# Gate, attention and state-space projections by tokens: 512 weight columns moving instead of 256 token columns

## The chip, the cores and the metric

The kernel runs on one core of a Trainium2 chip. The metric is the device time of one execution in microseconds, taken as the median of the runs. The engines are TensorE (PE in the profile; PEld is its weight load), VectorE (DVE), ScalarE (ACT), GpSimd (POOL) and SyncE (SP, which issues the loads).

## What is computed

One decoder block on 256 tokens of width 2048, in float32. Cut to the part around the change, the reference is:

```python
h = rms_norm(x, norm_mix_g) * (1.0 + sc1) + sh1          # sc1, sh1, g1, ... = silu(c) @ w_ada + b_ada
proj = h @ w_in                                          # (256, 8192)
u, q, k, v, ga, gb = split(proj, ...)                    # 1024 each; ga and gb 2048 each
y = gelu(s5_scan(u))                                     # state-space branch, (256, 1024)
y_ssm = y * sigmoid(y @ w_glu + b_glu)
y_att = attention(q, k, v, rel_bias)                     # 8 heads of 128, causal, (256, 1024)
merged = (sigmoid(ga) * (y_ssm @ w_proj_ssm)
          + sigmoid(gb) * (y_att @ w_proj_attn))         # (256, 2048)
x = x + g1 * (merged @ w_out)
h2 = rms_norm(x, norm_mlp_g) * (1.0 + sc2) + sh2
x = x + g2 * (square(relu(h2 @ w_ff1)) @ w_ff2)
out = rms_norm(x, norm_final_g)
```

## The kernel before

Every large product is computed in split precision. A weight tile of 128 rows (one k-tile of the contraction) by 1024 columns is loaded by SyncE (`load`, line 132) into one of seven `wraw` buffers. ScalarE casts it to the high part `whi` (line 137), and VectorE subtracts to get the low part `wlo` (line 139); there are four buffers of each. The activations are split in the same way (`xh`, `xl`). Three products then make one: high by high, low by high, high by low. Such a tile of 128 by 1024 with its matmuls is called a **unit** below.

There are two ways to run a unit on TensorE:

- `gemm_t` (lines 155 to 170) keeps 128 weight columns stationary and moves the 256 tokens. The result is transposed: features on the partitions, tokens along the free axis. A unit takes 8 column blocks by 3 products, which is 24 matmuls (lines 167, 168, 169) with 256 columns moving.
- `gemm_n` (lines 199 to 223) keeps 128 tokens stationary and moves 512 weight columns. The result has tokens on the partitions. A unit takes 2 token halves by 2 column halves by 3 products, which is 12 matmuls (lines 217, 218, 219) with 512 columns moving.

Either way the results fill four PSUM banks of 128 by 512 out of five (`mm`). Three more banks (`ax`) are for everything small.

The order of the work is that of the program, with priorities, put into a fixed instruction order per engine by a scheduler that simulates the kernel before it is built. Weight loads and splits get a higher priority (`OFF`). Work beside the large products sits in "lanes" (`lane`, `step`, lines 115 to 123): after each unit every lane may release so many jobs, at rates that are written as constants. The lane `ada` streams `w_ada` through the same `wraw` buffers and reduces it on VectorE (line 273). The lane `m` carries attention, then the state-space scan.

The order of the large products is: q, k, v, u and the first 1024 columns of gate a (`ga`) in three sweeps over the k-tiles (lines 986 to 993; `ga` takes ten k-tiles in the sweep of line 986 as `(4, 0, 1)` and six as `(4, 2, 2)`, both through line 960, with the partial sum in `gp`); the other three blocks of 1024 gate columns, 16 units each (lines 1023 to 1030), beside attention and then the state-space scan; `proj_attn(0)`, 8 units (lines 1044 to 1050); the GLU product, 8 units (line 1058); `proj_attn(1)`, 8 units; the state-space projection in two column groups of 8 units (lines 1072 to 1080); `w_out` by `gemm_n`, 2 times 16 units (line 1090). After it come the second norm and the feed-forward layers.

In the kernel before, all gate and projection results come from `gemm_t` and lie feature by token. The gates are copied out of PSUM by ScalarE (line 1029), or added by VectorE (line 925), and turned into sigmoids in the lane `sig` (line 1037). `proj_attn` multiplies each bank into `gb` (line 1048). The state-space branch keeps its tokens in another order (`s c` in place of `c s`), so the multiplication of the state-space projection into `ga` reads and writes with a stride (line 1078). Then `gb` is added (line 1079) and the sum is split into `mh` and `ml` (line 1080, which runs lines 137 and 139). As `mh` already has features on its partitions, `w_out` uses it as its stationary operand without further work.

## Time and profile before

| what | value |
|---|---|
| runs | 1430.0, 1430.75, 1433.79 us; median 1430.75 us |
| profiled execution, first to last instruction (span) | 1430.7 us, 24505 instructions |
| busy share | PE 97%, PEld 88%, DVE 73%, ACT 49%, POOL 3% |
| DMA | 353.47 MB, mean 247 GB/s |
| matmuls by `gemm_t`, all stages | 896 + 512 on each of lines 167, 168 and 169 by their largest groups |

The page gives the span of the profiled execution and no other time for it. The span lies 0.05 us under the median of the runs, so sums are made against 1430.7 us. Busy time on PE counts a matmul from its start to its modelled end, and neighbours overlap, so the distance from one matmul's start to the next says what a stream costs, and the mean duration does not. "Chain" means the chain of work that ended last, followed back from the end.

### The profile page before, as it was taken

Reading aid. Unit: us, or ns where it says so; the run is one execution under the profiler, and the core shown is the slowest. Engines: PE = TensorE matmul, PEld = TensorE weight load, DVE = VectorE, ACT = ScalarE, POOL = GpSimd, SP = SyncE. Lnnn points to the kernel's source line nnn. Section 1 sums busy time; section 2 is a strip of 40 time slices with the busy share of each in tenths; the row PEclk is TensorE's granted clock in tenths of the full one; section 3 lists DMA queues with packets and bytes.
Section 4 is the critical chain, followed back from the end, with each engine's and each line's share of the span. In section 5 each row is a group of like instructions: output and inputs, shape, how many; then the busy total and the mean of one; then the engine's idle time right before and its main releaser. Section 6 shows DMA issues by size and latency. Waiting matters only on the chain.

```text
span 1430.7 us, 24505 instructions
## 1 busy us (share of the span) xinstructions
PE 1386.5 (97%) x9866; PEld 1262.0 (88%) x9866; DVE 1041.2 (73%) x1435; ACT 702.4 (49%) x916; POOL 38.7 (3%) x89
## 2 busy tenths in 40 slices
PE   7789999999999999999899999999999999999996
PEld 6679899999999999988799998988888888888885
DVE  5588999977899788977685575667666555555676
ACT  4335353446636753445454564535363553635443
POOL 1000000310002100000000000000000000000000
PEclk9899999999999999999899999999999999999999
DMA  8999887697557988797497667768767566566561
GB/s 333 348 351 324 324 309 250 184 301 236 163 178 247 318 320 304 271 344 274 153 336 246 201 219 261 248 243 284 238 234 264 169 200 191 177 206 187 183 204 60
DMA packets 107218, 353.47 MB, mean 247 GB/s; under 512 B 12104, under 2 KB 12120, under 8 KB 106976
## 3 DMA queue, kind: packets, MB, share of 16 engines
q1 hardware_dynamic: 104240, 347.13, 71.6%
q0 software_dynamic: 2864, 4.78, 1.4%
q8 instruction: 77, 1.26, 0.3%
q14 instruction: 37, 0.30, 0.1%
HBM read 347.27 MB, written 2.49 MB: 244 GB/s over the span
## 4 chain that ended last, share of the span: by engine, by line
PE 88%; DVE 4%; DMA 4%; ACT 2%; issue 2%; SPq 0%; DVEq 0%; ACTq 0%
PE pt L167 13%; PE pt L169 13%; PE pt L168 13%; PE pn L217 11%; PE pn L219 11%; PE pn L218 11%; PE pw L193 8%; PE pw L195 4%; DMA wraw<-in_w_in_dram 3%; DVE wraw L273 1%; DVE wlo L139 1%; ACT whi L137 1%; PE adab L293 1%; PE ss L360 1%; PE ys L782 1%
## 5 line engine op out<-in xcount | busy, mean ns | idle before, releaser
L139 DVE TENSOR_TENSOR wlo<-wraw,whi 128x1024 fp32r<-128x1024 f32 x456 | 554.3, 1222 | 289.2 <-ACT whi L137 283.8
L137 ACT CAST whi<-wraw 128x1024 fp32r<-128x1024 f32 x456 | 475.8, 1050 | 582.8 <-PE pt L168 195.5
L167 PE MATMUL pt<-ah,whi 128*128 128x256 f32 x896 | 255.3, 291 | 9.3 <-ACT whi L137 5.8
L168 PE MATMUL pt<-ah,whi 128*128 128x256 f32 x896 | 252.0, 286 | 1.3 <-DVE ah L139 1.3
L169 PE MATMUL pt<-ah,wlo 128*128 128x256 f32 x896 | 243.2, 288 | 3.5 <-DVE wlo L139 3.4
L273 DVE SCALAR_TENSOR_TENSOR wraw<-wraw,cb 128x1024 f32<-128x1024 f32 x176 | 213.4, 1219 | 0.0
L218 PE MATMUL pn<-whi,ff 128*128 128x512 f32 x512 | 199.2, 389 | 0.0
L217 PE MATMUL pn<-whi,ff 128*128 128x512 f32 x512 | 197.9, 389 | 0.0
L167 PEld LDWEIGHTS pt<-ah,whi 128*128 128x128 f32 x896 | 173.1, 194 | 13.9 <-ACT whi L137 7.7
L219 PE MATMUL pn<-wlo,ff 128*128 128x512 f32 x512 | 185.3, 389 | 0.0
L193 PE MATMUL pw<-h2h,whi 128*128 128x512 f32 x512 | 178.3, 396 | 0.0
L168 PEld LDWEIGHTS pt<-ah,whi 128*128 128x128 f32 x896 | 173.8, 194 | 1.9 <-DVE ah L139 1.6
L169 PEld LDWEIGHTS pt<-ah,wlo 128*128 128x128 f32 x896 | 167.7, 194 | 5.3 <-DVE wlo L139 4.9
L167 PE MATMUL pt<-h2h,whi 128*128 128x256 f32 x512 | 144.6, 286 | 1.6 <-ACT h2h L137 1.1
L168 PE MATMUL pt<-h2h,whi 128*128 128x256 f32 x512 | 145.4, 285 | 0.0
L169 PE MATMUL pt<-h2h,wlo 128*128 128x256 f32 x512 | 144.2, 285 | 0.0
L195 PE MATMUL pw<-h2h,wlo 128*128 128x256 f32 x512 | 140.5, 279 | 0.0
L193 PEld LDWEIGHTS pw<-h2h,whi 128*128 128x128 f32 x512 | 95.2, 188 | 21.7
L219 PEld LDWEIGHTS pn<-wlo,ff 128*128 128x128 f32 x512 | 96.1, 188 | 20.1
L217 PEld LDWEIGHTS pn<-whi,ff 128*128 128x128 f32 x512 | 96.1, 188 | 19.8
L218 PEld LDWEIGHTS pn<-whi,ff 128*128 128x128 f32 x512 | 96.1, 188 | 19.7
L167 PEld LDWEIGHTS pt<-h2h,whi 128*128 128x128 f32 x512 | 98.7, 194 | 2.3 <-ACT h2h L137 1.5
(334 smaller groups left out, 1902.0 us busy)
## 6 DMA issues: line engine op xcount, KB each, us to landing
wraw<-in_w_ff_dram SPq DMA_DIRECT2D x256, 512.0 KB, 4.7
wraw<-in_wat_dram SPq DMA_DIRECT2D x176, 512.0 KB, 5.6
wraw<-in_w_in_dram SPq DMA_DIRECT2D x128, 512.0 KB, 5.3
wraw<-in_w_out_dram SPq DMA_DIRECT2D x32, 512.0 KB, 5.8
wraw<-in_wan_dram SPq DMA_DIRECT2D x16, 512.0 KB, 8.6
wraw<-in_w_proj_attn_dram SPq DMA_DIRECT2D x16, 512.0 KB, 7.1
wraw<-in_w_proj_ssm_dram SPq DMA_DIRECT2D x16, 512.0 KB, 5.6
wraw<-in_w_glu_dram SPq DMA_DIRECT2D x8, 512.0 KB, 6.2
```

The costliest lines, as they stand in the source:

```text
L137: h = self.nc.scalar.copy(hi, src)
L139: s = self.nc.vector.tensor_sub(lo, src, hi.bitcast(F32))
L167: nc.tensor.matmul(o, hi[:, c], xh[:, kx, :], start=st, stop=False, skip_group_check=True)
L168: nc.tensor.matmul(o, hi[:, c], xl[:, kx, :], start=False, stop=False, skip_group_check=True)
L169: self.mm = nc.tensor.matmul(o, lo[:, c], xh[:, kx, :], start=False, stop=sp, skip_group_check=True)
L193: nc.tensor.matmul(banks[b], hi[:, c], x2[:, k0 + k].rearrange("p h s -> p (h s)"), start=i + k == 0, stop=False, skip_group_check=True)
L195: self.mm = nc.tensor.matmul(banks[b][:, 0:S], lo[:, c], x2[:, k0 + k, 0, :], start=False, stop=i == n - 1 and k == 1, skip_group_check=True)
L217: nc.tensor.matmul(o, xh[:, kx, tk], hi[:, c], start=q == 0, stop=False)
L218: nc.tensor.matmul(o, xl[:, kx, tk], hi[:, c], start=False, stop=False)
L219: self.mm = last = nc.tensor.matmul(o, xh[:, kx, tk], lo[:, c], start=False, stop=q == n - 1)
L273: v.scalar_tensor_tensor(w, w, 1.0, self.cb[:, (i % 2) * 1024:(i % 2 + 1) * 1024], op0=OP.mult, op1=OP.mult, accum_out=pc[:, i:i + 1])
L293: self.nc.tensor.matmul(p[:, i * P:(i + 1) * P], cols[:, i:i + 1].to_broadcast([P, P]), self.ident, start=True, stop=True)
```

## The change

The gates, both halves of `proj_attn` and both of the state-space projection go from `gemm_t` to `gemm_n`. Their tiles `ga`, `gb` and `gp` change their shape to token by feature. `gemm_n` gets the `mid` hook that `gemm_t` had. In the GLU step the sigmoid now writes in natural token order, with a stride, and the multiplication by `yT` is strided; the state-space projection's multiplication no longer is. The merged result now has tokens on its partitions, so 128 by 128 blocks of it are transposed on TensorE into a small PSUM bank, four to a bank, and split from there into `mh` and `ml`. The diff, cut to its core:

```diff
-    def gemm_n(self, src, kts, c0, xh, xl, koff=0, tail=1):
+    def gemm_n(self, src, kts, c0, xh, xl, koff=0, tail=1, mid=None):
...
+            if mid and i == n // 2:
+                mid()
...
-                self.ga = self.slot("X16", [P, KT, S], name="ga")
+                self.ga = self.slot("X16", [P, 2, 2, 1024], name="ga")
...
-                    v.tensor_add(self.ga[:, s, :], gpart["p"][:, s, :], src)
+                    v.tensor_add(self.ga[:, 0, t, c], gpart["p"][:, t, c], banks[b])
...
-                g_evac(self.gemm_t(win, kts, 4096, self.ah, self.al, mid=mid), g0)
+                g_evac(self.gemm_n(win, kts, 4096, self.ah, self.al, mid=mid), g0)
...
-            banks = self.gemm_t(win, range(KT), c0, self.ah, self.al, mid=to_ssm if i == 1 else None)
+            banks = self.gemm_n(win, range(KT), c0, self.ah, self.al, mid=to_ssm if i == 1 else None)
             for b in range(4):
-                nc.scalar.copy(dst[:, (i % 2) * 8 + 2 * b:(i % 2) * 8 + 2 * b + 2, :],
-                               banks[b].rearrange("p (k s) -> p k s", s=S))
+                nc.scalar.copy(dst[:, i % 2, b // 2, (b % 2) * 512:(b % 2 + 1) * 512], banks[b])
...
-            banks = self.gemm_t(a["w_proj_attn"][0], range(8), cg * 1024, yh, yl)
+            banks = self.gemm_n(a["w_proj_attn"][0], range(8), cg * 1024, yh, yl)
...
+            tn = t.rearrange("p k (c s) -> p k s c", s=4)
             for k in range(2):
-                nc.scalar.activation(t[:, k], banks[b][:, k * S:(k + 1) * S], AF.Sigmoid,
-                                     bias=self.bglu[:, 2 * b + k:2 * b + k + 1])
+                nc.scalar.activation(tn[:, k], banks[b][:, k * S:(k + 1) * S].rearrange("p (s c) -> p s c", s=4),
+                                     AF.Sigmoid, bias=self.bglu[:, 2 * b + k:2 * b + k + 1])
-            v.tensor_mul(sc4(t), sc4(t), yT[:, s])
+            v.tensor_mul(tn, tn, yT[:, s])
...
-            banks = self.gemm_t(a["w_proj_ssm"][0], range(8), cg * 1024, gg[:, 0], gg[:, 1])
-            for b in range(4):
-                s = slice(cg * 8 + 2 * b, cg * 8 + 2 * b + 2)
-                d = ga[:, s, :]
-                dk = d.rearrange("p k (c s) -> p k s c", s=4)
-                v.tensor_mul(dk, dk, banks[b].rearrange("p (k s c) -> p k s c", k=2, s=4))
-                v.tensor_add(d, d, gb[:, s, :])
-                self.split(mh[:, s], ml[:, s], d)
+            banks = self.gemm_n(a["w_proj_ssm"][0], range(8), cg * 1024, gg[:, 0], gg[:, 1])
+            for b in (0, 2, 1, 3):
+                c = slice((b % 2) * 512, (b % 2 + 1) * 512)
+                d = ga[:, cg, b // 2, c]
+                v.tensor_mul(d, d, banks[b])
+                v.tensor_add(d, d, gb[:, cg, b // 2, c])
+                if b < 2:
+                    continue
+                for k in range(4 * (b % 2), 4 * (b % 2) + 4, 2):
+                    p = self.aux("trm")
+                    for j in range(2):
+                        for t in range(2):
+                            nc.tensor.transpose(p[:, j * S + t * P:j * S + (t + 1) * P],
+                                                ga[:, cg, t, (k + j) * P:(k + j + 1) * P], self.ident)
+                    s = slice(cg * 8 + k, cg * 8 + k + 2)
+                    self.split(mh[:, s], ml[:, s], p.rearrange("p (k s) -> p k s", s=S))
```

More of the change, by code (lines that the diff above doesn't have):

```diff
@@ L917, in g_evac @@
             if add:
-                self.ga = self.slot("X16", [P, KT, S], name="ga")
+                self.ga = self.slot("X16", [P, 2, 2, 1024], name="ga")
             else:
-                gpart["p"] = self.slot("S4", [P, 8, S], name="gp")
+                gpart["p"] = self.slot("S4", [P, 2, 1024], name="gp")
             for b in range(4):
-                s = slice(2 * b, 2 * b + 2)
-                src = banks[b].rearrange("p (k s) -> p k s", s=S)
+                t, c = b // 2, slice((b % 2) * 512, (b % 2 + 1) * 512)
                 if add:
-                    v.tensor_add(self.ga[:, s, :], gpart["p"][:, s, :], src)
+                    v.tensor_add(self.ga[:, 0, t, c], gpart["p"][:, t, c], banks[b])
                 else:
-                    nc.scalar.copy(gpart["p"][:, s, :], src)
+                    nc.scalar.copy(gpart["p"][:, t, c], banks[b])
         g1t = {}
@@ L994, in body @@
         ga = self.ga
-        self.asc = ga[:, 8:14, :].rearrange("p k s -> p (k s)").rearrange("p (i n) -> p i n", i=2)
+        self.asc = ga[:, 1].rearrange("p t n -> p (t n)")[:, 0:1536].rearrange("p (i n) -> p i n", i=2)
         self.yatt = self.slot("S5", [P, 8, S], name="yatt")
-        gb = self.slot("S1", [P, KT, S], name="gb")
+        gb = self.slot("S1", [P, 2, 2, 1024], name="gb")
         tabs = {}
@@ L1034, in sig @@
         def sig(t, q):
-            d = t[:, 4 * q:4 * q + 4, :].rearrange("p k s -> p (k s)")
+            d = t[:, q // 2, q % 2, :]
             with self.after(self.done[-1][1]):
@@ L1044, in proj_attn @@
         def proj_attn(cg):
-            banks = self.gemm_t(a["w_proj_attn"][0], range(8), cg * 1024, yh, yl)
+            banks = self.gemm_n(a["w_proj_attn"][0], range(8), cg * 1024, yh, yl)
             for b in range(4):
-                d = gb[:, cg * 8 + 2 * b:cg * 8 + 2 * b + 2, :].rearrange("p k s -> p (k s)")
+                d = gb[:, cg, b // 2, (b % 2) * 512:(b % 2 + 1) * 512]
                 v.tensor_mul(d, d, banks[b])
```

## The prediction, written before the changed kernel was run

> **What bounds the kernel now.** I read the page's first part, then the chain of waits by window, then the timeline.
>
> ```profile
> span 1430.7 us, 24505 instructions
> ```
> ```profile
> PE 1386.5 (97%) x9866; PEld 1262.0 (88%) x9866; DVE 1041.2 (73%) x1435; ACT 702.4 (49%) x916; POOL 38.7 (3%) x89
> ```
>
> TensorE is busy almost throughout. Whether it is the bound in the stages of the change is asked of the chain in three windows: 110 to 135 us, where the first ten k-tiles of the `ga` block run (its partial sum `gp` is copied there), 193 to 255 us with the other six, and 369 to 430 us, gates beside the scan.
>
> ```profile
> by line: DMA wraw<-in_w_in_dram 29.3%; DVE wlo L139 20.4%; issue 20.2%; DVE wraw L273 12.6%; DVE ah L139 7.6%; ACT gp L927 6.1%; ACT whi L137 4.5%; DVE xt L376 2.4%; DVE rt L581 2.3%; DVEq L139 0.4%; ACTq L137 0.2%
> ```
> ```profile
> 131.79 1.53 ACT gp L927 x3
> ```
> ```profile
> by line: PE pt L167 30.2%; PE pt L168 30.1%; PE pt L169 29.8%; PE trv L564 10.1%
> ```
> ```profile
> by line: PE pt L167 27.9%; PE pt L168 26.3%; PE pt L169 26.2%; PE ys L782 6.9%; PE vr L744 5.3%; PE vi L744 4.8%; PE ys L785 3.0%
> ```
> ```profile
> L925 DVE TENSOR_TENSOR ga<-gp,pt x4: 681/681/681, 242.9 to 247.0; 128x512 f32<-128x512 f32 x4
> ```
>
> In the first window nothing of TensorE is in the chain: loads, splits and reductions set the pace, and a faster product wins nothing. In the other two the chain is TensorE alone, with the three lines of `gemm_t` at 90% and 80%. The windows from 255 to 605 us answer like them, with lines of TensorE only. So the question is what a unit costs TensorE either way. The timeline of PE where the state-space projection (`pt`, 256 columns) goes over to `w_out` (`pn`, 512 columns) shows both; the first column is the start.
>
> ```profile
> 598.12 0.28 PE L168 MATMUL pt<-gg,whi 128*128 128x256 f32 x1
> 598.24 0.28 PE L169 MATMUL pt<-gg,wlo 128*128 128x256 f32 x1
> 598.36 0.40 PE L217 MATMUL pn<-whi,mh 128*128 128x512 f32 x1
> 598.59 0.40 PE L218 MATMUL pn<-whi,mh 128*128 128x512 f32 x1
> ```
> ```profile
> 1388.31 0.91 PE pn L219 x4
> ...
> 1410.07 0.91 PE pn L219 x4
> ```
>
> Starts lie 120 ns apart with 256 columns and about 230 ns with 512. The chain sharpens the second: the same place in two successive groups of 8 units (96 matmuls) is 21.76 us apart, so 226.7 ns each. Half as many matmuls of twice the width are not the same time: 2 x 120 - 226.7 = 13.3 ns fall away per pair.
>
> **The streams.** A unit goes from 24 x 0.120 = 2.880 us to 12 x 0.2267 = 2.720 us, 0.160 us less. The units are counted from the loads:
>
> ```profile
> wraw<-in_w_in_dram SPq DMA_DIRECT2D x128, 512.0 KB, 5.3
> ...
> wraw<-in_w_proj_attn_dram SPq DMA_DIRECT2D x16, 512.0 KB, 7.1
> wraw<-in_w_proj_ssm_dram SPq DMA_DIRECT2D x16, 512.0 KB, 5.6
> ```
>
> Half of the 128 are gates (4 of 8 column blocks): 64. Ten of them lie in the stage that TensorE does not bound. 54 + 16 + 16 = 86 units times 0.160 is **-13.8 us**.
>
> A rule of the Trainium skill speaks against this term. "TensorE: Matmul & The Clock Gate", section "Back-to-back issue gap", gives the gap as columns over 2.4 GHz plus about 2.5 ns, so a pair would save only 2.5 ns: as an estimate from that page, 86 x 12 x 2.5 ns = 2.6 us in all. The starts above differ from it.
>
> **The transposes.** 8 banks of 4 are 32 transposes of 128 x 128 float32. The nearest rows are the three of a head in attention, between matmuls of 256 columns.
>
> ```profile
> 313.99 0.28 PE L169 MATMUL pt<-ah,wlo 128*128 128x256 f32 x1
> 314.11 0.49 PE L670 MATMUL ptr<-ident,ga 128*128 128x128 f32 x3
> 314.36 0.36 PE L167 MATMUL pt<-ah,whi 128*128 128x256 f32 x1
> 314.56 0.28 PE L168 MATMUL pt<-ah,whi 128*128 128x256 f32 x1
> ```
> ```profile
> L670 PE MATMUL ptr<-ident,ga 128*128 128x128 f32 x24 | 5.0, 271 | 0.0
> ```
>
> From 313.99 to 314.56 are 0.57 us, of which two wide matmuls take 0.24: 0.33 us for three, 0.11 each. Without the slower restart it is 0.25/3 = 0.083; standing alone, the whole 271 ns. So 32 cost 2.7 to 8.7 us; I take 0.11, as the new ones also stand inside a stream: **+3.5 us**.
>
> **VectorE and ScalarE.** Evacuations keep number and shape. The strided multiplication moves from eight tiles of the merge to four of the GLU step.
>
> ```profile
> L1078 DVE TENSOR_TENSOR ga<-ga,pt 128x512 f32<-128x512 f32 x8 | 8.6, 1099 | 0.3 <-PE pt L169 0.3
> L1079 DVE TENSOR_TENSOR ga<-ga,gb 128x512 f32<-128x512 f32 x8 | 5.4, 686 | 0.0
> L1064 ACT ACTIVATE sg<-pt,cols 128x256 f32<-128x256 f32 x8 | 3.2, 485 | 0.0
> ```
>
> The merge saves 8 x (1.099 - 0.686) = 3.3 us of VectorE, the GLU pays 4 x (1.099 - 0.686) = 1.7 us if its multiplication runs at the 0.686 of the addition now. The strided write of the sigmoid costs between nothing and, if it slows as the multiplication does (1.6 times), 8 x 0.3 = 2.4 us of ScalarE. None is on the path: behind the GLU stand the 8 units of `proj_attn(1)`, 22 us; without that cover the 4 us would stand in front of the state-space projection.
>
> What can take gain back is that the other engines have to feed TensorE faster. Columns after the interval are its length and the busy time of PE, PEld, DVE, ACT and POOL (with counts), the clock, the DMA share and GB/s.
>
> ```profile
> 369.00:422.00 53.00, 53.00 (x716) 51.66 (x714) 52.26 (x70) 24.38 (x30) 0.00 (x0) 1.00 0.53 166
> ```
> ```profile
> 457.00:487.00 30.00, 30.00 (x253) 30.00 (x251) 22.89 (x30) 20.69 (x25) 11.48 (x24) 1.00 1.00 334
> ```
> ```profile
> ACT whi L137 <- PE pt L168: 12.3, 7, 4.0
> ```
>
> In the scan stage VectorE is as full as TensorE: 52.26 of 53 us. `gemm_t` takes 80% of it, 0.8 x 53 / 2.88 = 15 units, so up to 15 x 0.16 = 2.4 us of the gain can be lost there. But between 369 and 400 us the casts waited 12.3 us for TensorE to free a weight buffer: the four buffers were full, and the lead can be eaten instead. I take **+1.0 us**. From 457 to 487 us the DMA share is 1.00, over about 10 units: 0 to 1.6 us lost, and as seven raw buffers stand in between I take **+0.8 us**.
>
> **The new wait.** Before, TensorE needed nothing of the merge until `w_out`. Now transposes stand in its queue that wait for two multiplications and two additions on VectorE, and the casts of `mh` wait on ScalarE for the transposes, with weight casts queued behind them. Timelines of DVE (first and last merge step of each column group) and ACT:
>
> ```profile
> 573.36 1.12 DVE L1078 TENSOR_TENSOR ga<-ga,pt 128x512 f32<-128x512 f32 x1 [0.27 <-PE pt L169]
> ...
> 583.27 0.69 DVE L1079 TENSOR_TENSOR ga<-ga,gb 128x512 f32<-128x512 f32 x1
> ...
> 596.51 1.09 DVE L1078 TENSOR_TENSOR ga<-ga,pt 128x512 f32<-128x512 f32 x1
> ...
> 606.33 0.68 DVE L1079 TENSOR_TENSOR ga<-ga,gb 128x512 f32<-128x512 f32 x1
> ```
> ```profile
> 598.46 1.05 ACT L137 CAST whi<-wraw 128x1024 fp32r<-128x1024 f32 x1 [1.85 <-PE pt L168]
> ...
> 607.57 3.89 ACT L137 CAST whi<-wraw 128x1024 fp32r<-128x1024 f32 x4
> ```
>
> A merge runs 583.96 - 573.36 = 10.6 us and 607.01 - 596.51 = 10.5 us, mixed with splits. The next units cover it if the scheduler puts the transposes far enough behind them: the results are needed first by `w_out` (group 0) or at its ninth unit (group 1), 8 x 2.72 = 21.8 us later. Yet on ScalarE no weight cast starts between 598.46 and 607.57, 9.1 us, of the 4 x 2.72 = 10.9 us that four buffers hold: 1.8 us are left in group 1. I take **+1.5 us** for both groups, between 0 and 17 us (a rival, below).
>
> **Sum.** -13.8 + 3.5 + 1.0 + 0.8 + 1.5 = -7.0; 1430.7 - 7.0 = **1423.7 us**. What is saved is carried to the end, as the chain of `w_out` is TensorE too (605 to 692 us):
>
> ```profile
> by line: PE pn L219 31.6%; PE pn L218 31.0%; PE pn L217 31.0%; PE adab L293 3.3%; ACT xs L1098 0.8%; DVE x L1097 0.8%; DVE xs L1096 0.8%; DVE r2v L344 0.2%; DVE ss L1113 0.2%; issue 0.2%; ACT r2s L345 0.1%
> ```
>
> With the cheapest transposes and nothing taken back it is -13.8 + 2.7 = -11.1, 1419.6 us.
>
> **Rivals.** A, the feeders decide: all gate units from 369 to 487 us (118 us, some 34 units of 2.88) stay at the old pace, since VectorE or DMA was full there. These are 118 us with 80 to 100% `gemm_t`. Then 34 x 0.16 = 5.4 us are lost in place of 1.8: 1427.3 us. For it speaks the 52.26 of 53; against it the full weight buffers and that the next window has only 22.89 of 30 on VectorE.
>
> B, slower: the transposes are put close behind their product, and TensorE waits in its queue for the merge. A merge begins about 2 us before its product ends, so each group stands still for 10.6 - 2 = 8.6 us, two 17 us: 1430.7 - 13.8 + 3.5 + 17 = 1437.4 us. It turns slower than before from a wait of 5.2 us per group. For it speaks that VectorE is full around the merge and does it mixed with splits; against it, that the attention's transposes, which wait for ScalarE and VectorE too, show 0.0 idle time on PE.
>
> C, transposes at their full 271 ns: -13.8 + 8.7 + 1.8 + 1.5 = -1.8, 1428.9 us. The starts at 314.11 and 314.36 speak against it. In "PE-mode transpose" the same page of the Trainium skill has about 275 ns for one in a kernel, which would give an estimate of 32 x 0.275 = 8.8 us; the duration agrees, the cost in the stream does not.
>
> D, the width gives nothing here: the 13.3 ns do not belong to each matmul of these stages, so a pair of 256 costs what one of 512 does. Then nothing is saved, the feeders lose nothing, and the transposes are left: 1430.7 + 3.5 = 1434.2 us, short of 0.3%. `w_out`, with the same kinds of operands, speaks against it. By the rule of the Trainium skill's "Back-to-back issue gap" above it would be 2.6 us less, an estimate of 1431.6 us.
>
> **How the numbers follow.** A measurement of this kernel can tell about 0.3%, 4.3 us, from no change: below 1426.4 us is faster, above 1435.0 slower. The forecast has 0.62, A 0.20, B 0.11, C 0.04, D 0.03. Faster is the forecast, 0.62; A, C and D lie within 0.3%, 0.27; slower is B, 0.11. The forecast's own range is 1419.6 to 1426.4. For 8 in 10 the range takes in A and C and nearly all of D: 1419 to 1432 us; it leaves out B and a little at each end.
>
> **What would show it.** Matmuls on `pn` from the gates on, 227 ns from start to start; 1032 fewer matmuls in the stages that TensorE binds; from the end of the last k, v product to the first matmul of `w_out` some 7 us less; 32 transposes on tile `trm` with a cost near 0.11 us each and little idle time before them. Idle time on PE before `trm`, released by VectorE's additions, of 5 us or more per group would make it wrong as B; waits of `pn` for `wlo` or `whi` between 369 and 487 us would make it wrong as A.

## The result and the profile after

The changed kernel takes 1442.8 us in the median (1438.74 to 1444.09), the kernel before 1430.74 us on the same chip: the ratio is 1.0081, with a 95% interval of 1.0068 to 1.0094. It is slower by about 12 us; 7 us less was forecast. The profiled execution took 1442.36 us with a span of 1440.5 us, 9.8 us longer than before's span. (In every run on record a span is 1.7 to 2.0 us shorter than the time of its execution. Before's span of 1430.7 us, the base of the sum, so belongs to an execution some 1.7 us above before's median, and 9.8 and 12 us do not contradict each other.) Line numbers from `gemm_n` on are two higher than before's (its matmuls are now lines 219 to 221, the `w_ada` reduction is line 275, the scan's product with the states line 784, the merge lines 1078 and 1079). The transposes are line 1086.

The page's first rows, and the chain's shares by engine:

```profile
span 1440.5 us, 22275 instructions
...
PE 1381.8 (96%) x8746; PEld 1201.9 (83%) x8746; DVE 1038.1 (72%) x1435; ACT 701.4 (49%) x916; POOL 38.7 (3%) x89
...
PE 78%; DVE 10%; DMA 7%; issue 2%; ACT 2%; SPq 0%; DVEq 0%; ACTq 0%
```

There are 1120 matmuls fewer, but the busy time of PE fell by only 4.7 us, and the span grew. The last row shows where the time went: the chain, which was TensorE alone from 193 us to `w_out`, now runs through VectorE and the loads. The same view of the kernel after in three windows (369 to 430, 457 to 500 and 500 to 520 us):

```profile
by line: DVE wlo L139 11.6%; PE pn L219 10.1%; PE pn L220 9.0%; PE pn L221 8.6%; issue 8.1%; DVE rw L763 5.8%; DVE wraw L275 5.6%; PE vr L746 3.5%; DVE rw L768 3.2%; PE vi L746 3.1%; DVE rw L753 2.3%; DVE rw L750 2.3%; DVE rw L754 2.1%; DVE
...
by line: DMA wraw<-in_w_proj_attn_dram 21.7%; DVE wraw L275 12.6%; PE pn L219 11.6%; PE pn L220 11.5%; PE pn L221 10.0%; issue 9.8%; ACT whi L137 7.4%; DVE wlo L139 7.2%; DVE gt L797 3.0%; DVE yy L139 3.0%; ACT gt L798 1.5%; DVE u L800 1.4%
...
by line: DMA wraw<-in_w_glu_dram 36.6%; DVE wlo L139 11.5%; issue 11.4%; PE pt L167 10.0%; PE pt L168 8.2%; DVE wraw L275 6.8%; DVE yy L139 6.2%; PE pt L169 6.2%; ACT whi L137 5.3%; ACTq L137 0.2%
```

Where before these windows held lines of TensorE alone, now splits, `w_ada` reductions and weight loads decide. Note the third: the GLU product is still `gemm_t`, so its own matmuls are no faster. Its loads come later because of what stands ahead of them.

Which section loses how much is read from the starts of the stages: VectorE's first addition into `ga`, then the first matmul of each later stage (starts rounded to 0.1 us). "Ideal" is before's length less 0.160 us for each unit that went over to `gemm_n`, plus 0.11 us for each transpose.

| stage | before | ideal | after | lost |
|---|---|---|---|---|
| gates, from the addition into `ga` to `proj_attn(0)` (48 units) | 240.3 | 232.6 | 241.5 | 8.9 |
| `proj_attn(0)` (8) | 23.0 | 21.7 | 27.1 | 5.4 |
| GLU and `proj_attn(1)` (8) | 46.1 | 44.8 | 48.8 | 4.0 |
| state-space projection (16, and 16 transposes) | 46.1 | 45.3 | 48.0 | 2.7 |
| `w_out` and second norm (16 transposes) | 99.0 | 100.8 | 100.9 | 0.1 |
| from the addition into `ga` to the first feed-forward matmul | 454.5 | 445.2 | 466.3 | 21.1 |

Up to the addition 0.8 us were won (no more than scatter: the old form with the same rates up to there, four kernels, reaches it between 240.7 and 242.9 us), and behind the feed-forward's start 1.2 us: 466.3 - 454.5 - 0.8 - 1.2 = 9.8 us, the difference of the spans. So the gain is there, and about 21 us of loss are on top of it. The view of waits for PE in the kernel after shows the first part of it; here are the largest groups between 360 and 565 us (total, times, longest):

```profile
PE ys L784 <- DVE sri L769: 3.1, 2, 1.7
PE pn L219 <- ACT whi L137: 3.0, 3, 1.7
PE ys L784 <- DVE sri L772: 2.6, 2, 1.5
PE pt L167 <- ACT whi L137: 1.8, 1, 1.8
PE pn L219 <- ACT ga L1030: 1.1, 2, 0.6
PE pn L221 <- DVE wlo L139: 1.1, 2, 0.5
```

From 245 to 565 us the idle gaps of PE add up to 14.3 us, each under 1.8 us; before there was none. The row from 245 to 565 us of before, then of after (its length, then the busy time of PE, PEld, DVE, ACT and POOL, the granted clock, DMA share and GB/s):

```profile
245.00:565.00 320.00, 320.00 (x3342) 313.29 (x3340) 274.20 (x395) 175.03 (x253) 33.04 (x68) 1.00 0.75 245
```
```profile
245.00:565.00 320.00, 305.69 (x2409) 261.45 (x2409) 262.07 (x378) 168.77 (x246) 33.01 (x68) 0.98 0.71 233
```

The second part of the loss does not show as idle time at all. Here are PE's timeline behind the waits at 431 and 433 us, and stretches of 2 and 4 us there, in the same columns:

```profile
433.13 0.33 PE L784 MATMUL ys<-sri,cc 64*64 64x64 f32 x2 [1.49 <-DVE sri L772]
433.38 0.50 PE L219 MATMUL pn<-whi,ah 128*128 128x512 f32 x1
433.72 0.39 PE L220 MATMUL pn<-whi,ah 128*128 128x512 f32 x1
...
434.81 0.63 PE L221 MATMUL pn<-wlo,ah 128*128 128x512 f32 x1
435.23 0.63 PE L219 MATMUL pn<-whi,ah 128*128 128x512 f32 x1
...
437.79 0.43 PE L219 MATMUL pn<-whi,ah 128*128 128x512 f32 x1
```
```profile
430.00:434.00 4.00, 1.20 (x9) 0.94 (x10) 3.96 (x7) 0.00 (x0) 0.00 (x0) 1.00 0.15 57
434.00:436.00 2.00, 2.00 (x7) 1.61 (x6) 2.00 (x3) 0.00 (x0) 0.00 (x0) 0.61 0.00 0
436.00:438.00 2.00, 2.00 (x6) 1.53 (x5) 1.97 (x4) 1.04 (x1) 0.00 (x0) 0.54 0.70 188
438.00:440.00 2.00, 2.00 (x28) 1.46 (x29) 2.00 (x4) 0.82 (x1) 0.00 (x0) 1.00 0.18 74
```

After 2.8 us of idle time in 4, TensorE works without a gap, but at half the clock. Starts lie 0.42 us apart in place of 0.227, and the eight matmuls up to 437.79 us lose about 1.6 us. The same happens behind the waits at 488.58 us (granted clock 0.50 from 490 to 492) and 515.25 us (0.59 and 0.56 from 516 to 520). By the starts the first two cost 1.6 us each and the third, with 256 columns (0.213 us apart in place of 0.120), 1.5 us: 4.7 us. Gaps and clock together are 14.3 + 4.7 = 19.0 of the 21.1 us.

The chain of the kernel after shows how the wait at 488.58 us comes about (start, length, what):

```profile
476.89 1.16 DVE wraw L275 x2
478.05 0.02 issue
478.07 9.32 DMA wraw<-in_w_proj_attn_dram
487.38 0.02 issue
487.40 0.04 ACTq L137
487.44 0.04 issue
487.48 1.05 ACT whi L137
488.54 0.04 issue
488.58 0.50 PE pn L219
```

A reduction of the `w_ada` lane ends on VectorE, which frees a raw buffer. Only then does SyncE issue the load of the next `proj_attn` tile, which takes 9.32 us to land; the DMA share is 1.03 from 478 to 487.4 us. Cast and matmul follow at once. Those two streams share seven raw buffers, and each unit of `proj_attn` now takes TensorE 2.72 us in place of 2.88.

### The profile page after: what moved, and what is told of

Read it like the earlier page. It is cut to its first block, busy times and chain, and to the rows that moved or that the text cites. A ratio compares the mean times of both kernels' runs of the same rounds, so it can differ in the third digit from the quotient of the medians.

```text
span 1440.5 us, 22275 instructions
## 1 busy us (share of the span) xinstructions
PE 1381.8 (96%) x8746; PEld 1201.9 (83%) x8746; DVE 1038.1 (72%) x1435; ACT 701.4 (49%) x916; POOL 38.7 (3%) x89
## 4 chain that ended last, share of the span: by engine, by line
PE 78%; DVE 10%; DMA 7%; issue 2%; ACT 2%; SPq 0%; DVEq 0%; ACTq 0%
PE pn L219 14%; PE pn L220 14%; PE pn L221 14%; PE pw L193 8%; PE pt L167 7%; PE pt L168 7%; PE pt L169 7%; PE pw L195 4%; DVE wlo L139 3%; DVE wraw L275 3%; DMA wraw<-in_w_in_dram 3%; ACT whi L137 1%; DMA wraw<-in_w_proj_attn_dram 1%; DMA wraw<-in_w_proj_ssm_dram 1%; PE ss L362 1%
## 5 line engine op out<-in xcount | busy, mean ns | idle before, releaser
L219 PE MATMUL pn<-whi,ah 128*128 128x512 f32 x320 | 127.0, 399 | 2.8 <-ACT whi L137 1.5
L220 PE MATMUL pn<-whi,ah 128*128 128x512 f32 x320 | 126.1, 395 | 0.0
L167 PE MATMUL pt<-ah,whi 128*128 128x256 f32 x384 | 108.5, 291 | 8.6 <-ACT whi L137 4.6
L221 PE MATMUL pn<-wlo,ah 128*128 128x512 f32 x320 | 114.1, 397 | 0.9 <-DVE wlo L139 0.9
L193 PEld LDWEIGHTS pw<-h2h,whi 128*128 128x128 f32 x512 | 95.3, 188 | 21.7
L168 PE MATMUL pt<-ah,whi 128*128 128x256 f32 x384 | 108.0, 287 | 1.9 <-DVE ah L139 1.3
L169 PE MATMUL pt<-ah,wlo 128*128 128x256 f32 x384 | 102.3, 288 | 1.9 <-DVE wlo L139 1.8
```

Source lines behind the costliest of these rows:

```text
L167: nc.tensor.matmul(o, hi[:, c], xh[:, kx, :], start=st, stop=False, skip_group_check=True)
L168: nc.tensor.matmul(o, hi[:, c], xl[:, kx, :], start=False, stop=False, skip_group_check=True)
L169: self.mm = nc.tensor.matmul(o, lo[:, c], xh[:, kx, :], start=False, stop=sp, skip_group_check=True)
L193: nc.tensor.matmul(banks[b], hi[:, c], x2[:, k0 + k].rearrange("p h s -> p (h s)"), start=i + k == 0, stop=False, skip_group_check=True)
L219: nc.tensor.matmul(o, xh[:, kx, tk], hi[:, c], start=q == 0, stop=False)
L220: nc.tensor.matmul(o, xl[:, kx, tk], hi[:, c], start=False, stop=False)
```

## Experiments: is it the feeding?

**Theory F.** The faster products outrun what feeds them: VectorE in the scan, and loads and raw buffers in the projections, both shared with the `w_ada` stream. **Rivals.** M: the token order itself costs the time (merge, transposes, evacuations). O: the fixed order of the instructions does, however much capacity there is. The stage lengths below come from one profiled execution of each run, which can lie some 4 us off the median beside it (us; the state-space column ends with `w_out`'s first matmul):

| kernel | gates | proj_attn(0) | GLU, proj_attn(1) | state-space | w_out, norm | median |
|---|---|---|---|---|---|---|
| before | 240.3 | 23.0 | 46.1 | 46.1 | 99.0 | 1430.7 |
| after | 241.5 | 27.1 | 48.8 | 48.0 | 100.9 | 1442.8 |
| e1_late_before | 240.1 | 23.0 | 46.1 | 46.1 | 104.5 | 1436.8 |
| e1_late_after | 236.1 | 21.7 | 44.9 | 45.4 | 105.4 | 1437.5 |
| e2_no_transposes | 242.1 | 25.7 | 45.6 | 41.4 | 99.8 | 1432.8 |
| e3_scan_slower | 239.2 | 28.6 | 48.5 | 46.1 | 100.9 | 1438.4 |
| e4_scan_unloaded | 239.1 | 23.5 | 48.8 | 47.5 | 100.8 | 1436.9 |
| e5_projections_unloaded | 239.7 | 21.8 | 44.8 | 45.4 | 100.9 | 1430.2 |
| e6_ada_earlier | 253.2 | 21.8 | 44.8 | 45.4 | 100.9 | 1441.6 |
| e7_half | 241.6 | 24.1 | 44.9 | 41.2 | 104.4 | 1431.2 |
| e8_idle_before | 240.9 | 30.2 | 55.2 | 53.8 | 99.1 | 1456.1 |
| e9_mild_after | 235.8 | 21.7 | 44.9 | 45.4 | 104.2 | 1431.2 |
| e10_mild_before | 240.5 | 23.0 | 46.1 | 46.1 | 105.5 | 1435.0 |
| e11_attention_faster | 238.6 | 21.7 | 45.0 | 45.4 | 100.9 | 1430.3 |
| e12_scan_hook_earlier | 244.8 | 21.8 | 44.9 | 45.6 | 101.2 | 1439.9 |
| e13_evacuate_on_vector | 245.5 | 21.8 | 44.8 | 45.4 | 100.9 | 1433.2 |
| e14_both_less_ada | 245.4 | 21.8 | 44.8 | 45.4 | 103.4 | 1436.9 |
| e15_less_ada_in_scan | 245.3 | 21.7 | 44.8 | 46.0 | 102.1 | 1435.8 |
| e16_after_no_late_stream | 248.8 | 21.7 | 44.9 | 45.4 | 100.8 | 1437.1 |
| e17_before_no_late_stream | 243.9 | 23.0 | 46.1 | 46.1 | 99.0 | 1434.6 |

The lane rates are released jobs per unit: `RS0`, `RS1` and `RS2` for `w_ada` beside attention, the scan and the last gate block, `RPA` beside the projections, `RWO` and `RM` behind them; `RAT` is attention's, `RSS` the scan's. The diffs are cut to the lines that matter.

**e1: the `w_ada` jobs later, in both kernels.**

```diff
-RS1 = .25
-RS2 = .7
-RPA = .65
-RWO = .45
-RM = .72
+RS1 = 0.0
+RS2 = .35
+RPA = .5
+RWO = .8
+RM = .95
```

> The kernel before with the same moved ada work: the control. TensorE had no idle time from 374 to 600 us there, so F expects nothing to win, 1429 to 1434 us. If it wins several us too, the rates and not the pairing with the change are what e1_late_after shows. With F, e1_late_after lies 4 to 10 us below this one; with O or M 8 to 12 us above it.

> The changed kernel with 18 of the ada loads and reductions moved out of the scan, gate and projection stages into w_out and the first feed-forward product (lane rates in the scan stage 0 for .25, in the last gate stage .35 for .7, in the projections .5 for .65, then .8 for .45 and .95 for .72). Theory F (TensorE now outruns VectorE in the scan and the loads in the projections; the idle time lets its clock drop): most of the 19 us between the 10.3 us that streams and transposes should save and the 9.8 us lost comes back, 1422 to 1430 us, and the stretches at half clock at 434, 490 and 516 us go. Rival O (the new fixed order as such is bad, and the load of the feeders does not matter): no systematic change, 1438 to 1446 us. Rival M (merge and transposes cost it): no change, 1443 us.

The changed kernel took 1437.54 us (1.0048 [1.0033, 1.0063] of before), the kernel before at the same rates 1436.84 us (1.0049 [1.0032, 1.0066]). The pair differs by 0.7 us where the original pair differs by 12. The three projection stages of the changed kernel became the ideals within 0.1 us (21.7, 44.9, 45.4), and the gates came to 236.1; from the addition to `w_out`'s first matmul the changed kernel is now 7.1 us shorter than its partner. The stages of before did not move up to there: TensorE was the bound, with or without the load. Both kernels take 4.5 to 5.5 us longer in `w_out`, where the jobs now are, and from the feed-forward's first matmul on the changed one takes 737.7 us for 732.1 and the kernel before 734.4 for 733.3. So both times missed what was expected of them (1422 to 1430 and 1429 to 1434 us): the gain came where theory F put it and was lost behind it. Up to `w_out` the load matters, and only to the changed kernel.

**e2: the transposes left out** (the splits read the merged tile directly, so `mh` and `ml` hold other elements than they should).

```diff
-                    p = self.aux("trm")
-                    for j in range(2):
-                        for t in range(2):
-                            nc.tensor.transpose(p[:, j * S + t * P:j * S + (t + 1) * P],
-                                                ga[:, cg, t, (k + j) * P:(k + j + 1) * P], self.ident)
-                    self.split(mh[:, s], ml[:, s], p.rearrange("p (k s) -> p k s", s=S))
+                    f = k // 4
+                    self.split(mh[:, s], ml[:, s], ga[:, cg, k // 2 % 2, f * 512:(f + 1) * 512].rearrange("p (k s) -> p k s", s=S))
```

> The changed kernel without the 32 transposes: mh is split straight from ga, so the values that w_out gets are not the merged result transposed. F: saves the 32 x 0.11 = 3.5 us of TensorE and little else, 1438 to 1440 us. M: saves 10 us or more, 1433 us or less. O: cannot be told, since the order changes again.

It took 1432.82 us, 1.0014 [0.9999, 1.0028] of before and 10 us under the changed kernel, far more than 32 transposes by their starts. By its size that is what rival M expected (1433 us or less); its profiled execution was its fastest, 1428.87 us. The stage boundary moves here (without transposes `w_out` can begin inside the last units), so the state-space and `w_out` columns are taken together: 141.2 us, against 146.3 in e5, where nothing waits in them. That is 5.1 us or 0.16 us for each transpose, and 148.9 - 146.3 = 2.6 us that the changed kernel loses by waiting there. By the profiles another 4.6 us lie in `proj_attn(0)` and the GLU stage, ahead of every transpose: there the waits became shorter, for a reason that this run does not show (the order of the instructions is another one, too). So this run alone does not exclude M; behind the gates e5 does, which keeps the transposes and has no loss there.

**e3 and e4: relieve the scan.** e3 lets the scan's jobs out more slowly, e4 stops `w_ada` beside it.

```diff
-RSS = .43
+RSS = .36
```

> The changed kernel with the scan's jobs spread over 39 units in place of 33 (lane rate .36 for .43). F: VectorE is less dense per unit in the scan stage, so the waits of the ys products at 413 to 433 us (6 us, and the 1.7 us of half clock behind them) get smaller: 3 to 7 us less than 1443 us, unless the end of the scan then holds up the GLU. O and M: within 3 us of 1443 us.

```diff
-RS1 = .25
+RS1 = 0.0
```

> The changed kernel with no ada work in the scan stage alone (that lane rate 0 for .25, the rest as changed). F: the gates reach their end (first matmul of proj_attn) at 478 to 481 us in place of 483.6, as in e1_late_after (478.8); the projections lose as before; 1436 to 1441 us. O: no systematic effect.

e3 took 1438.41 us (1.0051 [1.0035, 1.0066]) and e4 1436.9 us (1.0046 [1.0029, 1.0063]). The gates came down by about 2.4 us in both, of 8.9 that are lost there. In e3 the projections stayed as bad as in the changed kernel. In e4 `proj_attn(0)` recovered most of its loss, and the two stages behind it did not. e3's gain is what was expected of it; e4 should have reached `proj_attn(0)` at 478 to 481 us and did at 483.7. The load beside the scan explains a part of the gates' loss, and in e4 also most of `proj_attn(0)`'s, though not that of the two stages behind it.

**e5: relieve the last gate block and the projections.**

```diff
-RS2 = .7
-RPA = .65
+RS2 = .35
+RPA = .5
```

> The changed kernel with less ada work in the last gate stage and the projections alone (.35 for .7 and .5 for .65). F: from the first matmul of proj_attn to the first of w_out 112 to 117 us in place of 123.9 (e1_late_after: 112.0), with the scan stage as slow as in the changed kernel; 1431 to 1437 us. O: no systematic effect.

It took 1430.21 us, 0.9997 [0.9987, 1.0007] of before and 12.6 us under the changed kernel. The three projection stages are 21.8, 44.8 and 45.4 us, the ideals within 0.1 us. The chain from 457 to 500 us, then from 560 to 580 us, in this run:

```profile
by line: PE pn L219 33.8%; PE pn L220 33.7%; PE pn L221 32.7%
...
by line: PE pn L220 34.1%; PE pn L221 33.0%; PE pn L219 32.8%; PE trm L1086 1.6%
```

The loads, reductions and splits that filled these windows in the changed kernel are gone from the chain. The same instructions of TensorE now run without a stop: the loss in the projections is the `w_ada` stream running beside them at the old rate.

**e6: the same jobs earlier,** beside attention.

```diff
-R3 = .5
-RS0 = .7
-RS1 = .25
-RS2 = .7
-RPA = .65
-RWO = .45
+R3 = .7
+RS0 = 1.0
+RS1 = 0.0
+RS2 = .5
+RPA = .5
+RWO = .5
```

> The changed kernel with ada work moved the other way, into the stages before the scan, where VectorE and DMA had room (rates .7 for .5 in the last sweep, 1.0 for .7 beside attention), and out of the scan (0 for .25), the last gate stage (.5 for .7) and the projections (.5 for .65); w_out gets .5 for .45. F: the gain of e1_late_after up to w_out without its later loss: 1420 to 1430 us, below the kernel before if the sweep and attention stages stay bound by TensorE. O: 1435 to 1445 us.

It took 1441.58 us (1.0078 [1.0063, 1.0093]): the projections are ideal again, but the gates grew to 253.2 us, 11.7 more than in the changed kernel. 1420 to 1430 us was expected. This placement ahead of the projections gains nothing; that the load itself lengthens the gates is not shown by it, as e15 and e16 below have less load there and longer gates too.

**e7: only the second 1024 columns by tokens** (of both gates and both projections).

```diff
+            gemm = self.gemm_n if i % 2 else self.gemm_t
...
+            gemm = self.gemm_n if cg else self.gemm_t
```

> Half the change: only the second 1024 columns of both gates, of proj_attn and of the state-space projection by tokens (48 of the 96 units, none of them in the scan stage, and 16 of the 32 transposes); the first 1024 as before, in natural token order. F: -7.7 + 1.8 us from streams and transposes, and losses in the projections alone: 1425 to 1433 us. O: half of the loss, about 1436 us.

It took 1431.18 us, 1.001 [0.9998, 1.0021] of before. Half of the change costs nothing measurable, and gains nothing. The first projection stage is 24.1, longer than before's 23.0 although it is still `gemm_t`: at 484.04 us it waits 0.37 us for `whi`, and its next matmuls start further apart. That fits a lead of the loads that the faster gates ahead of it have eaten, but nothing here shows it.

**e8: what does an idle moment cost?** The kernel before, with five stops of TensorE, one in each of the five products from `proj_attn(0)` on: a chain of narrow matmuls and ScalarE copies that wait for one another.

```diff
+        for _ in range(n):
+            p = self.aux("idp")
+            with self.after(self.mm):
+                self.mm = nc.tensor.matmul(p[:, 0:64], self.ident, src, start=True, stop=True)
+            nc.scalar.copy(x, p[:, 0:64])
+            src = x
...
+            gate = self.idle(idle) if idle and i == 4 else None
```

> The kernel before with five stops put into TensorE's queue, one in the middle of each product from proj_attn(0) to the second state-space projection: three round trips of a small matmul, a ScalarE copy and the next matmul, with the product's matmuls behind them; the feeders go on. Tests the half-clock part of theory F. If an idle stretch only costs its own length, the time grows by the five idle stretches as the profile shows them (about 3 us each, 15 us). If the clock drops behind each, every stretch costs 1.7 us more (3.4 us at half clock), some 23 us in all, and the granted clock reads near 0.5 behind each stop.

It took 1456.12 us (1.0186 [1.0168, 1.0203]). The five stages grew by 7.2 + 9.1 + 7.7 = 24.0 us. PE's visible idle time in the stops is 9.5 us, 3.2 in the first and 1.6 in each of the others. Four of the five stops were followed by a stretch at half clock. The fourth was not, and took 3.0 us (578.53 to 581.53 us), idle time and narrow matmuls together. At that price, and 1.7 us more idle time in the first, five stops take 16.7 us; some 7 us are left for the clock. So the 23 us expected were met partly by luck: the idle time was 9.5 and not 15 us, and the stops' own matmuls made up for it. The first stop's timeline and its stretch, and the fourth stop's:

```profile
496.11 0.69 PE L163 MATMUL idp<-idx,ident 128*128 128x64 f32 x2 [2.62 <-ACT idx L164]
...
579.82 0.43 PE L163 MATMUL idp<-idx,ident 128*128 128x64 f32 x2 [0.96 <-ACT idx L164]
```
```profile
498.00:502.00 4.00, 3.91 (x18) 3.91 (x19) 0.00 (x0) 0.04 (x1) 0.00 (x0) 0.50 0.95 357
...
582.00:586.00 4.00, 4.00 (x36) 4.00 (x35) 0.36 (x1) 1.05 (x1) 0.00 (x0) 1.00 1.00 375
```

In four microseconds after the first stop 18 matmuls ran, two of them the stop's own narrow ones; after the fourth 36. So the clock's part of the loss is reproduced in a kernel that has none of the change: behind a stop with 1.6 to 3.2 us of idle time, 3.41 us at half clock hold 16 matmuls of 256 columns, which take 1.92 us at full clock. That is 1.5 us more, or nothing where, as behind the fourth, the clock stays.

**e9 and e10: e1 in a milder form, in both kernels.**

```diff
-RS1 = .25
-RS2 = .7
-RPA = .65
-RWO = .45
+RS1 = 0.0
+RS2 = .35
+RPA = .5
+RWO = .6
```

> The changed kernel with e1's relief of the scan, gates and projections (0, .35, .5) but only .6 in w_out and the old .72 in the feed-forward product, where e1 lost 4.5 and 5 us. F: gates as in e1_late_after (478.8 us), projections 112.0 us, w_out about 102 us: 1424 to 1429 us, the first version below the kernel before. O: 1435 us or more.

> The kernel before with the same rates as e9_mild_after, the control: up to w_out as before (TensorE had no idle time), in w_out 1 to 3 us more: 1430 to 1434 us. F: e9_mild_after lies 4 to 9 us below it; that difference is what the change is worth where the feeders keep up (10.1 us by streams and transposes).

The changed kernel took 1431.16 us (1.0008 [0.9998, 1.0018]), the kernel before 1434.95 us (1.0034 [1.0022, 1.0046]). At equal rates the change is now worth 3.8 us in the medians, just short of the 4 to 9 expected. From the addition to `w_out`'s first matmul it is 347.8 against 355.7 us, 7.9 less; but e9's profiled execution was its fastest (1427.1 us) and e10's lies 1.9 us above its median, so the stages show where the gain lies better than how large it is. The rates that let it gain cost 3.3 and 6.5 us in `w_out` (104.2 and 105.5 us). Against the kernel before as it was nothing is left, where 1424 to 1429 us was expected of e9.

**e11 to e15: the rest of the gates' loss,** each on top of e5. e11 lets attention run ahead, e12 moves the hook that starts the scan to a quarter of the block, e13 copies the first block's banks on VectorE in place of ScalarE, e14 does both with less `w_ada` work, e15 has only that.

```diff
-RAT = 1.5
+RAT = 2.0
```

> e5_projections_unloaded with the attention's jobs released faster (lane rate 2.0 for 1.5), as in the changed kernel the scan's first matmul came 10 us later (377 for 367 us) after attention ended later, and VectorE stood idle for 8 of the 12 us before it. If this late start is what costs the gates their 7.7 us, the scan starts earlier, proj_attn at 478 to 481 us for 484, and the time is 1424 to 1428 us. If the scan stage is short of VectorE either way, proj_attn starts at 483 to 485 us and the time stays at 1430 us.

```diff
-            if mid and i == n // 2:
+            if mid and i == n // at:
...
+            banks = self.gemm_n(win, range(KT), c0, self.ah, self.al, mid=to_ssm if i == 1 else None, at=4)
```

> e5_projections_unloaded with the hook that ends attention and starts the scan at the fourth unit of its gate block in place of the eighth. Start theory (the gates lose their gain because attention ends and the scan starts late, at 377 us for 367): the scan starts by 370 us, proj_attn at 477 to 480 us for 484, 1422 to 1427 us. Capacity theory (the scan stage has not enough VectorE for units of 2.72 us): proj_attn stays at 482 to 485 us, 1429 to 1432 us.

```diff
-                nc.scalar.copy(dst[:, i % 2, b // 2, (b % 2) * 512:(b % 2 + 1) * 512], banks[b])
+                (v.tensor_copy if i == 1 else nc.scalar.copy)(dst[:, i % 2, b // 2, (b % 2) * 512:(b % 2 + 1) * 512], banks[b])
```

> e5_projections_unloaded with the copies of the gate block beside attention out of PSUM on VectorE, which stood idle there, in place of ScalarE, where they queued behind attention and tables. If the banks held so long (weight casts stop from 361 to 376 us) are what costs the gates, the casts go on, proj_attn starts at 479 to 482 us for 484, 1425 to 1428 us. Capacity theory: 483 to 485 us, 1429 to 1432 us.

```diff
-RS1 = .25
+RS1 = .1
```

> Both of the above, and the ada rate in the scan stage .1 for .25. Start or bank theory: proj_attn at 475 to 479 us, 1420 to 1425 us. Capacity theory: the lower rate alone frees 15 x 0.15 x 1.3 = 3 us of VectorE, proj_attn at 480 to 483 us, 1427 to 1430 us.

> e5_projections_unloaded with the ada rate in the scan stage .1 for .25 alone. Capacity theory: proj_attn at 480 to 482 us for 484, 1426 to 1429 us; this is the version meant to beat both kernels. Start and bank theories: 484 us, 1430 us.

Against before they are 0.9996 [0.9986, 1.0007], 1.0063 [1.0048, 1.0079], 1.0017 [1.0008, 1.0026], 1.0039 [1.0025, 1.0054] and 1.0033 [1.0023, 1.0043]. The projections stay ideal in all five, so everything happens in the gates: 238.6 in e11, and 244.8 to 245.5 us in the others, 5 to 6 us more than in e5. e12 has one wait of 6.00 us of the scan's last product for its input (released by ScalarE's copy into `u`), e15 one of 6.80 us for a low part `wlo` at 436.8 us. e15 speaks against capacity: less load on VectorE beside the scan, and more time lost. e13 speaks against the copies: with that block's copies off ScalarE the weight casts still stop, from 363.1 to 378.5 us. The start of the scan was not tested: its first matmul comes at 379.4 us in e12 and 377.1 in e11, against 379.6 in e5, so neither edit brought it near the 367 us of before (e11, at 483.0 us and 1430.3 us, fits what a lack of VectorE expected). No theory of one cause for the gates is shown so far.

**e16 and e17: the later `w_ada` stream taken out of both kernels.**

```diff
+            if vec >= 2:
+                return
...
+            if vec >= 2:
+                v.tensor_copy(pc[:, i:i + 1], self.half)
+            else:
```

> The changed kernel with the later part of the w_ada stream left out (its loads and VectorE reductions for g1, sc2, sh2 and g2; a fixed number stands in their place, so the output is another). The other work, the scan's 50 us of VectorE among it, stays. Theory (the faster products outrun what feeds them, and the w_ada stream takes the share of VectorE, DMA and raw buffers that they lack): between the first matmul of the ga addition and w_out's first matmul nearly all of the 20.8 us of loss go, so that this kernel is 7 to 10 us shorter there than the kernel before with the same part left out (-13.8 + 3.7 = -10.1), and its median is 7 to 11 us under that kernel's. TensorE's idle time from 245 to 500 us falls from 11.2 to under 3 us. Rival 1 (the scan alone overfills VectorE, or the fixed order of the instructions is at fault, whatever the load): the gates keep a loss of 5 to 9 us, only the projections recover, and the two kernels differ by 1 to 5 us. Rival 2 (the loss is in the token order itself): they differ by +8 to +12 us as the unchanged pair does.

> The kernel before with the same later part of the w_ada stream left out, as the partner of the run above. TensorE was busy all the time from 245 us to w_out in the kernel before, so both theories expect the same stages there as before within 2 us (gates 240.3, proj_attn(0) 23.0, GLU and proj_attn(1) 46.1, state-space projection 46.1 us), and a median within 5 us of the kernel before; if it is much shorter, the stream cost TensorE time before too, and the pair has to be compared, not each with its own original.

e16 took 1437.06 us (1.0046 [1.0031, 1.0062]), e17 1434.63 us (1.0033 [1.0021, 1.0046]): e16 is 2.4 us the slower, where my theory had it 7 to 11 us the faster and rival 1 had 1 to 5 us between them. The theory, that nearly all of the loss would go, failed for the gates and held for the projections. These are ideal within 0.1 us without any change of a rate. The gates got longer in both kernels with less to do, 248.8 and 243.9 us, and from 245 to 500 us e16 still has 9.5 us of idle time on TensorE, of 11.2 in the changed kernel. The wait that makes up most of it, on PE's timeline of e16, and VectorE's timeline up to the split that it waits for:

```profile
430.34 0.39 PE L220 MATMUL pn<-whi,ah 128*128 128x512 f32 x1
437.38 0.79 PE L221 MATMUL pn<-wlo,ah 128*128 128x512 f32 x1 [6.65 <-DVE wlo L139]
```
```profile
426.97 1.22 DVE L139 TENSOR_TENSOR wlo<-wraw,whi 128x1024 fp32r<-128x1024 f32 x1
428.10 0.68 DVE L755 TENSOR_TENSOR rw<-vr,tbl 128x512 f32<-128x512 f32 x1
...
435.50 0.68 DVE L773 TENSOR_TENSOR rw<-rw,tbl 128x504 f32<-128x504 f32 x1
436.10 1.22 DVE L139 TENSOR_TENSOR wlo<-wraw,whi 128x1024 fp32r<-128x1024 f32 x1
```

The cast for that split was done by 427.74 us, and the split itself takes 1.2 us. But in VectorE's fixed order eleven steps of the scan stand between it and the split before, 8 us of work. TensorE waits 6.65 us, and a stretch at half clock follows (granted 0.91 over the 40 us from 420 to 460). VectorE has room in the same stretch: it is busy for 30.68 of those 40 us. This is shown for e16: there it is the order and not the capacity. e15's wait is alike: fifteen other VectorE instructions stand between two splits, from 425.16 to 435.55 us. In the changed kernel itself VectorE is idle ahead of the scan and full in it. Here are two windows of before, then of after:

```profile
360.00:380.00 20.00, 20.00 (x257) 19.35 (x256) 17.41 (x24) 13.51 (x20) 0.00 (x0) 1.00 0.42 128
380.00:420.00 40.00, 40.00 (x518) 39.12 (x516) 39.83 (x53) 18.57 (x23) 0.00 (x0) 1.00 0.62 193
```
```profile
360.00:380.00 20.00, 18.29 (x140) 14.93 (x139) 7.92 (x16) 15.81 (x32) 0.00 (x0) 1.00 0.17 54
380.00:420.00 40.00, 37.49 (x364) 30.61 (x364) 39.97 (x54) 17.14 (x23) 0.00 (x0) 1.00 0.62 201
```

The third number group is VectorE. At the hand-over from attention to the scan it has 7.92 us of work in 20, against 17.41 before; the scan's first matmul comes at 377.0 us and not at 366.7. Behind it, it is as full as before, and TensorE loses 2.5 us in 40. What puts these instructions so was not isolated. The gates of the variants wholly by tokens lose between 3 us (e9) and 21 us (e6).

## Why the prediction was wrong

The mechanism of the streams was right. By the starts, 86 units should save 13.8 us. In e5 and e16 `proj_attn(0)`, with 8 units, takes 21.7 to 21.8 us against 23.0: 0.16 us each. Rival D is out. So is the saving of 2.6 us in all by the Trainium skill's formula for the isolated gap ("TensorE: Matmul & The Clock Gate", section "Back-to-back issue gap").

The transposes were right too. They stand in the stream with no idle time ahead of them, nine of them in 0.90 us here, and cost 1.9 us in `w_out`'s stage (16). By e2 all 32 come to about 5.1 us, against 3.5 taken and bounds of 2.7 to 8.7. The group row and a piece of the timeline of the kernel after:

```profile
L1086 PE MATMUL trm<-ident,ga 128*128 128x128 f32 x32 | 4.8, 272 | 0.0
```
```profile
594.70 1.15 PE L1086 MATMUL trm<-ident,ga 128*128 128x128 f32 x9
595.60 0.48 PE L220 MATMUL pn<-whi,gg 128*128 128x512 f32 x1
```

With that B is out: no idle time before `trm`. B was the only rival that forecast a slower kernel, so none foresaw this result for the reason that held. The new wait, taken at 1.5 us, hardly exists: in e5, where nothing else waits, the state-space projection, `w_out` and the norm take 45.4 + 100.9 = 146.3 us, and the ideals are 45.3 + 100.8 = 146.1. VectorE's part went as worked out, with the merge's multiplication at 684 ns and the GLU's strided one at 1090; the sigmoid's strided write took 715 ns for 485, 1.8 of the 2.4 us allowed for it:

```profile
L1078 DVE TENSOR_TENSOR ga<-ga,pn 128x512 f32<-128x512 f32 x8 | 5.1, 684 | 0.7 <-PE pn L221 0.7
...
L1068 DVE TENSOR_TENSOR sg<-sg,yT 128x512 f32<-128x512 f32 x4 | 4.2, 1090 | 0.0
```

The step that failed is the pair of feeder terms, "I take +1.0 us" for VectorE in the scan stage and "I take +0.8 us" for the loads from 457 to 487 us, and with them the price of rival A. The signs and the places were right: `pn` and `pt` do wait for `wlo` and `whi`. The gates lost 8.9 us and the stages from `proj_attn(0)` to `w_out` 12.1: 21 us where these terms had 1.8. The mechanism was rival A's, at four times its 5.4 us and over a longer stretch. Three things were wrong in the sizing:

- Both bounds assumed that a feeder that was full before keeps its old pace, so that the worst case is to gain nothing (2.4, 1.6, and 5.4 us in A). Nothing in the profile said so. A VectorE that is full shows that the order fits the old pace, and the gates after are slower than before in spite of the faster products.
- The interval was too short. The DMA share of 1.00 was read from 457 to 487 us and priced for ten units, but `proj_attn(0)`, GLU, `proj_attn(1)` and the state-space projection lost 12.1 us up to `w_out`, the GLU product without being changed. A lead of the loads that is spent early and missing later would do that; what e5 shows is that a slower `w_ada` stream gives it all back.
- No stop was priced above its idle time. Three of them let the clock drop, 1.5 to 1.6 us each, 4.7 of the 21 us; e8 shows the same in a kernel without the change.

One sentence on the range does not fit its own sums: D stands at 1434.2 us, and a range that ends at 1432 us leaves it out.

What of the cause is shown: for the projections, that the `w_ada` stream beside them takes what feeds them (e1, e5, e6 and e16 slow it or leave it out, and the loss is gone); which of its shares, DMA, raw buffers or VectorE, weighs most was not separated. For the gates' 8.9 us, that waits for `sri`, `wlo` and copies are there, and that order alone can make them (e16, e17, e15). That the scheduler's fixed order is what makes the changed kernel's own gate loss is argued and not shown. More raw buffers were not tried.

## What to carry to other kernels

When a product is made faster in a kernel where TensorE is busy all the time, ask not only which engine is full beside it, but how much lead each feeder has and what other stream shares its buffers; slow that stream with the same edit, or the gain can turn into stops. Price a stop of TensorE above its idle time, since the clock may drop behind it. And judge such a change beside a partner with the same rates (here 3.8 us won), and then against the kernel as it was (nothing won): the second answers the question.

## What the runs showed of the hardware that was not expected

The clock drops behind short stops. In the changed kernel single gaps of 1.67 and 1.49 us close together, and one of 1.76 us at 515.25 us, were followed by about 3.4 us at a granted clock near 0.5 (434.4 to 437.8 us). In e8 a stop with 1.56 to 1.61 us of idle time did so three times in four. Where the idle time falls matters too: by the clock records of the traces, the slow stretches of one execution start on a grid. In the changed kernel they begin at 434.44, 489.06 and 516.36 us, 16 and 8 steps of 3.413 us apart, and in the step just before each PE was idle for 1.77, 2.20 and 1.76 us. In e8 the fourth stop's 1.56 us fell on two steps, 1.26 and 0.30 us, and nothing followed; the other four put 1.40 to 2.06 us into one step. In the twenty traces, from 180 to 720 us, no step at full clock with less than 1.40 us of idle time was followed by half clock, every one with more than 1.92 us was, and in between both happened. "TensorE: Matmul & The Clock Gate" of the Trainium skill, section "Part 1: The HAM clock gate", says that half clock follows an idle window of about 3.4 us. The length of the slow stretch agrees with that window; the idle time that sets it off here is about half of it, within one step of the grid, and the measurement decides.

At half clock the advantage of the wide matmul is gone: starts are 0.426 us apart with 512 columns (434.81 to 437.79 us, seven steps) and 0.213 us with 256 (e8, 499.12 to 502.10 us, fourteen steps), two to one, where at full clock a pair of narrow ones costs 0.240 us against 0.2267. So a slow stretch of 3.41 us takes 1.6 us from the changed form and 1.5 us from the old one.
